# An encoder layer on one core: the down projection with tokens on the partitions, the up projection's products summed in their banks, group statistics in a transposes' bank

## The chip, the cores and the metric

One core of a Trainium2 chip runs the whole layer in one launch. The metric is the device time of one execution in microseconds (us). The kernel before was timed three times: 2064.53, 2067.25 and 2067.41 us, median 2067.25.

## The reference, cut to what matters

S = 512 tokens of D = 2048 channels; D_FF = 5632. All in float32. The change concerns the second half of the layer, the gated MLP and what ends it:

```
x = x + einsum("bsc,cd->bsd", mixed, w_out)          # out projection, residual
xn = rms_norm(x, ffn_norm_g)
up = einsum("bsd,df->bsf", xn, w_up)                 # 2048 -> 2 x 5632
up = depthwise_conv(up, ffn_dw_w, ffn_dw_b)          # width 3 over the tokens
gate, val = split(up, 2)
x = x + einsum("bsf,fd->bsd", silu(gate) * val, w_down)   # 5632 -> 2048
out = rms_norm(x, final_norm_g)
```

The first half (in projection, a convolution group and a neighbourhood attention group, each normalised, then the out projection) is touched in one place only: the banks in which two of its statistics are summed.

## The kernel before, in words

**Precision.** Every float32 operand is used as a sum of two parts, hi + lo, and a product is three matmuls: hi·hi, hi·lo, lo·hi. ACT makes the hi part (`whi`, L117, a copy of 1024 columns), DVE the lo part (`wlo`, L118, a subtraction). `weights()` runs a plan of weight units of 512 KB, `AHEAD` = 3 units ahead of their use: SP loads a unit into one of `NR` = 7 `raw` tiles (L112), then ACT and DVE split it. All engines take their instructions in order; a list scheduler fixes that order when the kernel is built, from priorities (the order of writing, shifted for the background `steps` that `tick` hands out) and from the tiles that are free. Nearly all intermediate tiles of 128x512 come from one pool of `NT` = 79 slots (`t2`), 56 of which hold the 28 combinations of the input through the whole MLP; a new tile waits until the last reader of the slot's old tile is done, be that reader an engine or a DMA.

**Up projection.** It goes through 44 blocks f of 128 gate and 128 value channels. For f >= 4 a block is seven products (a fast scheme for 2x2 blocks: seven half-size products instead of eight, over the halves of the channels and of the tokens). A product is 8 steps over k, each a matmul of 512 columns (L692, `whi` against [hi | lo] of 256 tokens) and one of 256 (L693, `wlo` against hi, into the upper half). So a bank of a product holds two halves, main and low. Each product has a bank of its own: products 0 to 5 go through the three "mm" banks, product 6 uses "po". ACT copies nine quarters of 256 columns out (`vv`, `pl`, L706) and DVE does eleven additions and two multiplications by the row statistic `rstd2` to make gate and value (L721 to L745, L788, L789). A conv of width 3 (`uy`, L780 to L782), silu (L791) and a product (L792) give the hidden block. Blocks f < 4 (`up_apart`) do the same with matmuls of 256.

**Down projection.** Four blocks make a chunk; there are 11. The hidden blocks of chunk c-1, split into `hh` and `hl`, wait in `pend` and are used while chunk c is made: a weight unit after product 3 of a block and one after product 6 (`down_units`). The weights are stationary and the tokens move: a unit holds the weights of two output blocks d, each takes 4 x 3 matmuls of 512 columns (L128 to L130) in a "tr" bank, ACT copies the bank to `pdc` (L812) and POOL adds it to the residual `xd[d]` in DRAM by an accumulating DMA of 256 KB (L813). Of a block's four such DMAs two follow product 3 and two product 6.

**The end.** In the last chunk the remaining eight d of `pend` run in one piece while the last weights are split into `dh`, `dl` (L839, L840) and the residual is loaded back into `x2`. Then `half(h0)` does the last chunk's contribution for the first 256 tokens, all 16 d, matmuls of 256 columns; `half(h1)` the other 256 tokens, with the statistic of the first half in between: 8 matmuls (L183) that sum the squares over the channels, which lie on the partitions, and 2 (L200) that spread the result over the partitions again. The first half's output is scaled and written in the shadow of the second half (`first_half`), the second half's after the last matmul.

**Statistics.** `rsqrt_steps` and the LayerNorm's mean (L389) take their bank from "sc", the bank pair of the attention scores.

Of the kernel before, what the change touches and what calls it, by code (L numbers as in the profile page):

```python
# [16 lines left out]
P = 128  # L17
D = 2048
# [22 lines left out]
H = S // 2  # L41
CH = 4
NCH = NF // CH
NT = 79
NR = 7
AHEAD = 3
# [13 lines left out]
         ("nag", NC_), ("g2", KD), ("fww", 2 * NF * 3), ("fwb", 2 * NF), ("g3", KD)]  # L60
# [9 lines left out]
def layer(ctx: ExitStack, tc: tile.TileContext, xT, w_in, w_v, w_out, w_up, w_down, par, tab, out):  # L70
# [20 lines left out]
    def t4(shape, name):  # L91

        return wpool.tile(shape, F32, tag="raw", name=name, bufs=NR)

# [70 lines left out]
    def sum_sq(acc, src, first, to=slice(0, S)):  # L165
        if first:
            nc.scalar.activation(acc, src, AF.Square)
        else:
            q = t2("sq")[:, to]
            nc.scalar.activation(q, src, AF.Square)  # L170
            nc.vector.tensor_add(acc, acc, q)

    def rsqrt_steps(accs, n, name, to=slice(0, S), keep=True, col=None):

        if not isinstance(accs, tuple):
            accs = accs,
        m = (to.stop - to.start) // P
        bank = lambda: (psa.tile([P, 2, S], F32, tag="sc", name="st")[:, 0] if col is None else
                        psa.tile([P, S], F32, tag="po", name="st"))
        ps = bank()  # L180
        for i in range(m):
            for acc in accs:
                nc.tensor.matmul(ps[:, i:i + 1], acc[:, to.start + i * P:to.start + (i + 1) * P], ones[:, 0:1],  # L183
                                 start=acc is accs[0], stop=acc is accs[-1])
        v, r, y = (sm.tile([P, S // P], F32, tag="rs" + c, name="rs" + c)[:, :m] for c in "vry")
        nc.vector.tensor_scalar(v, ps[:, :m], 1.0 / n, EPS, op0=ALU.mult, op1=ALU.add)
# [4 lines left out]
        nc.vector.scalar_tensor_tensor(y, y, 1.5, r, op0=ALU.add, op1=ALU.mult)  # L191
        if col is not None:
            nc.vector.tensor_copy(col, y)
# [6 lines left out]
        nc.tensor.matmul(ps[:, :m * P], ones, dg[:, :m * P], start=True, stop=True)  # L200
        if not keep:
            return ps[:, :m * P]
        res = t2(name)
        nc.scalar.activation(res[:, to], ps[:, :m * P], AF.Copy)
        return res

    def rsqrt_value(g):
        while True:
            try:
                next(g)  # L210
            except StopIteration as e:
                return e.value
# [165 lines left out]
    def group_a():  # L378
# [9 lines left out]
        ps = psa.tile([P, 2, S], F32, tag="sc", name="st")[:, 0]  # L388
# [194 lines left out]
    def after(d, ps):  # L583
# [26 lines left out]
        for c, f in enumerate((t4_, t1, t3, b11, t2_, b21, b22)):  # L610
            halves(f, c)
# [17 lines left out]
    def factors(f):  # L629
# [5 lines left out]
        def make(c):  # L635
            if c == 0:
                return load(A22)
            if c == 1:
                a["s"] = t4([P, U * P], "ws")
                add(a["s"], load(A21), a[A22])  # L640
            elif c == 2:
                add(a[A21], a[A21], load(A11))
                return a[A21]
            elif c == 3:
                return a[A11]
            elif c == 4:
                add(a["s"], a["s"], a[A11])
# [12 lines left out]
    def down_units(c, i, at):  # L660

        n = U // CH
# [4 lines left out]
        return {(1, 3): (0,), (1, 6): (2,), (2, 3): (4,), (2, 6): (6,), (3, 6): range(8, KD, n)}.get((i, at), ())  # L667

    def down_weights(f0, d0):
        return w_down[:, (f0 * KD + d0 * CH) * P:(f0 * KD + d0 * CH + U) * P]  # L670

    for c in range(NCH):
        for i in range(CH):
            for at, make in enumerate(factors(c * CH + i)):
                plan.append(make)
                for d0 in down_units(c, i, at):
                    plan.append(lambda c=c, d0=d0: unit(down_weights((c - 1) * CH, d0), U * P))
# [4 lines left out]
    def up(f, between):  # L682

        def product(c):

            w = weights()
            ps = (psa.tile([P, S], F32, tag="po", name="pu") if c == 6 else
                  psm.tile([P, S], F32, tag="mm", name="pu"))
            for k in range(U):
                hi, lo = (w[i][:, k * P:(k + 1) * P] for i in range(2))  # L690
                m = comb[c][k]
                wide = lambda: nc.tensor.matmul(ps, hi, m, start=k == 0, stop=k == U - 1)  # L692
                low = lambda: nc.tensor.matmul(ps[:, H:], lo, m[:, :H], start=False, stop=False)  # L693

                if k < U - 1:
                    wide()
                    i = low()
                else:
                    low()
                    i = wide()  # L700
            tick(i)
            between(c)
            return ps[:, :H], ps[:, H:]
# [4 lines left out]
        def pair(name):  # L708
            return t2(name).rearrange("p (i t) -> p i t", i=2)

        def both(x):
            return x.unsqueeze(1).broadcast_to([P, 2, H])


        vv, low = pair("vv"), pair("pl")
        for i in range(2):
            m, l = product(i)
            copy(vv[:, i], m)
            copy(low[:, i], l)
        m7, l = product(2)  # L720
        add(vv, vv, low)  # L721
        low = pair("pl")
        copy(low[:, 0], l)
        m1, l = product(3)
        copy(low[:, 1], l)
        uu, v = pair("uu"), pair("vl")
        u, u2 = uu[:, 0], uu[:, 1]
        add(u2, m7, low[:, 0])
        add(v, vv, both(u2))
        m6, l = product(4)  # L730
# [238 lines left out]
```

## Time and profile before

| | us |
|---|---|
| the three runs | 2064.53, 2067.25, 2067.41 |
| the profiled execution, its own time | 2063.7 |
| its span, first to last instruction | 2061.9 |
| TensorE (PE) busy | 2040.6 (99%) |
| VectorE (DVE) busy | 1652.3 (80%) |
| ScalarE (ACT) busy | 1057.5 (51%) |
| GpSimd (POOL) busy, nearly all of it issuing DMAs | 156.6 (8%) |
| mean granted TensorE clock | 0.997 |

The profiled execution is 3.55 us below the median of the three runs. Matmuls overlap, so the time that a matmul costs is the distance between the starts of two of them in the timeline, not its duration. The same goes, by about 0.1 us each, for DVE and ACT instructions that follow one another without a wait.

### The profile page before, as it was taken

Reading aid. Unit: us, or ns where it says so; the run is one execution under the profiler, and the core shown is the slowest. Engines: PE = TensorE matmul, PEld = TensorE weight load, DVE = VectorE, ACT = ScalarE, POOL = GpSimd, SP = SyncE. Lnnn points to the kernel's source line nnn. Section 1 sums busy time; section 2 is a strip of 40 time slices with the busy share of each in tenths; the row PEclk is TensorE's granted clock in tenths of the full one; section 3 lists DMA queues with packets and bytes.
Section 4 is the critical chain, followed back from the end, with each engine's and each line's share of the span. In section 5 each row is a group of like instructions: output and inputs, shape, how many; then the busy total and the mean of one; then the engine's idle time right before and its main releaser. Section 6 shows DMA issues by size and latency. Waiting matters only on the chain.

```text
span 2061.9 us, 28498 instructions
## 1 busy us (share of the span) xinstructions
PE 2040.6 (99%) x10746; PEld 1726.8 (84%) x10746; DVE 1652.3 (80%) x2285; ACT 1057.5 (51%) x1714; POOL 156.6 (8%) x186
## 2 busy tenths in 40 slices
PE   9999999999999999999999999999999999999997
PEld 7888888777888998888888888888888888888887
DVE  7798893975577898888888888788788887889876
ACT  7223423466536555555555555555554554555562
POOL 0000000000001001111111111111111111110110
PEclk9999999999999999999999999999999999999998
DMA  6532234325447435555465555555555565554572
GB/s 242 163 103 92 93 115 151 103 72 184 136 144 187 117 123 141 126 143 144 117 150 143 131 135 143 135 131 143 136 134 143 129 144 142 131 137 123 148 210 82
DMA packets 103338, 281.68 MB, mean 137 GB/s; under 512 B 12064, under 2 KB 16672, under 8 KB 103200
## 3 DMA queue, kind: packets, MB, share of 16 engines
q1 hardware_dynamic: 77840, 233.70, 35.7%
q0 software_dynamic: 25216, 46.15, 14.9%
q8 instruction: 85, 1.39, 0.3%
q14 instruction: 53, 0.43, 0.1%
q10 hardware_dynamic: 144, 0.01, 0.0%
HBM read 223.18 MB, written 56.62 MB: 136 GB/s over the span
## 4 chain that ended last, share of the span: by engine, by line
PE 89%; DVE 4%; DMA 3%; issue 2%; ACT 1%; POOL 0%; SPq 0%; DVEq 0%; POOLq 0%; ACTq 0%
PE pu L692 23%; PE pu L693 12%; PE pd L130 8%; PE pd L128 8%; PE pd L129 8%; PE pj L128 5%; PE pj L129 5%; PE pj L130 5%; PE po L128 2%; PE po L129 2%; PE po L130 2%; PE pv L315 1%; PE pv L314 1%; PE pv L316 1%; DMA sq<-sq 1%
## 5 line engine op out<-in xcount | busy, mean ns | idle before, releaser
L692 PE MATMUL pu<-xc,whi 128*128 128x512 f32 x2240 | 782.6, 397 | 0.2 <-ACT pl L706 0.2
L118 DVE TENSOR_TENSOR wlo<-raw,whi 128x1024 fp32r<-128x1024 f32 x364 | 444.7, 1222 | 247.6 <-ACT whi L117 232.1
L117 ACT ACTIVATE whi<-raw 128x1024 fp32r<-128x1024 f32 x364 | 385.1, 1059 | 470.5 <-PE pj L129 130.3
L693 PE MATMUL pu<-xc,wlo 128*128 128x256 f32 x2240 | 583.0, 281 | 0.0
L692 PEld LDWEIGHTS pu<-xc,whi 128*128 128x128 f32 x2240 | 407.8, 188 | 80.3 <-ACT pl L706 0.5
L693 PEld LDWEIGHTS pu<-xc,wlo 128*128 128x128 f32 x2240 | 422.8, 189 | 25.5
L130 PE MATMUL pd<-hh,wlo 128*128 128x512 f32 x640 | 248.9, 391 | 1.4 <-DVE wlo L118 1.4
L128 PE MATMUL pd<-hh,whi 128*128 128x512 f32 x640 | 249.8, 390 | 0.0
L129 PE MATMUL pd<-hl,whi 128*128 128x512 f32 x640 | 249.1, 389 | 0.0
L813 POOL DMA_DIRECT2D x2d<-pdc x160 | 139.6, 874 | 1174.0 <-ACT pdc L812 1072.1
L128 PE MATMUL pj<-xh,whi 128*128 128x512 f32 x512 | 200.5, 396 | 0.2 <-ACT xh L244 0.2
L129 PE MATMUL pj<-xl,whi 128*128 128x512 f32 x512 | 200.4, 391 | 0.1
L130 PE MATMUL pj<-xh,wlo 128*128 128x512 f32 x512 | 200.4, 391 | 0.0
L706 ACT ACTIVATE pl<-pu 128x256 f32<-128x256 f32 x280 | 105.1, 380 | 176.1 <-PE pu L692 176.1
L117 ACT ACTIVATE whi<-ws 128x1024 fp32r<-128x1024 f32 x132 | 139.8, 1059 | 68.5 <-PE pu L692 44.3
L372 DVE SCALAR_TENSOR_TENSOR y<-ch,prm,y 128x510 f32<-128x510 f32 (+14 forms) x240 | 172.0, 743 | 3.5
L118 DVE TENSOR_TENSOR wlo<-ws,whi 128x1024 fp32r<-128x1024 f32 x132 | 161.1, 1220 | 1.4 <-ACT whi L117 1.3
L130 PEld LDWEIGHTS pd<-hh,wlo 128*128 128x128 f32 x640 | 120.1, 188 | 30.0 <-DVE wlo L118 4.9
L812 ACT ACTIVATE pdc<-pd 128x512 f32<-128x512 f32 x160 | 93.9, 588 | 95.4 <-PE pd L130 95.4
L129 PEld LDWEIGHTS pd<-hl,whi 128*128 128x128 f32 x640 | 120.2, 188 | 25.7
L128 PEld LDWEIGHTS pd<-hh,whi 128*128 128x128 f32 x640 | 120.4, 188 | 21.8
L128 PEld LDWEIGHTS pj<-xh,whi 128*128 128x128 f32 x512 | 96.3, 188 | 25.0 <-issue 3.8
(176 smaller groups left out, 2913.7 us busy)
## 6 DMA issues: line engine op xcount, KB each, us to landing
raw<-in_w_up SPq DMA_DIRECT2D x176, 512.0 KB, 3.6
raw<-in_w_down SPq DMA_DIRECT2D x88, 512.0 KB, 3.6
x2d<-pdc POOLq DMA_DIRECT2D x160, 256.0 KB, 4.5
raw<-in_w_in SPq DMA_DIRECT2D x60, 512.0 KB, 3.7
raw<-in_w_out SPq DMA_DIRECT2D x32, 512.0 KB, 3.7
x<-in_xT SPq DMA_DIRECT2D x32, 256.0 KB, 4.3
raw<-in_w_v SPq DMA_DIRECT2D x16, 512.0 KB, 4.8
tab<-in_tab SPq DMA_DIRECT2D x32, 256.0 KB, 4.0
```

Source lines behind the costliest of these rows:

```text
L117: i = nc.scalar.activation(hi[:, :n], raw[:, :n], AF.Copy)
L118: j = nc.vector.tensor_sub(lo[:, :n], raw[:, :n], hi[:, :n].bitcast(F32))
L128: nc.tensor.matmul(ps, hi[:, a], mh, start=start, stop=False)
L129: nc.tensor.matmul(ps, hi[:, a], ml, start=False, stop=False)
L130: return nc.tensor.matmul(ps, lo[:, a], mh, start=False, stop=stop)
L314: nc.tensor.matmul(ps[i], xh, w[0][:, a], start=kk == 0, stop=False)
L372: nc.vector.scalar_tensor_tensor(y[:, a:b], h[:, a + j - PAD:b + j - PAD], prm[:, o + j:o + j + 1], y[:, a:b], op0=ALU.mult, op1=ALU.add)
L692: wide = lambda: nc.tensor.matmul(ps, hi, m, start=k == 0, stop=k == U - 1)
L693: low = lambda: nc.tensor.matmul(ps[:, H:], lo, m[:, :H], start=False, stop=False)
L706: nc.scalar.activation(to, ps, AF.Copy)
L812: nc.scalar.activation(t, ps, AF.Copy)
L813: nc.gpsimd.dma_start(xd[d], t, accum_op=ALU.add)
```

## The change: what it does

1. **Down projection turned round.** The hidden block is now the stationary operand (128 tokens of it), the weights move (512 columns), and a bank holds 128 tokens x 512 output channels. A unit is a quarter `a` of the output channels and half of a chunk's four blocks. Four banks (two "tr", "po", one "mm") are opened at the unit after product 3 and closed at the unit after product 6; only then come four `pdc` copies and four POOL DMAs in a row, into a new DRAM buffer `xq[a][i]` (i: token tile). The first of these writes does not add. The count of copies, DMAs and matmuls stays.
2. **The residual is turned** once, by `turn_residual`, a background step from chunk 1 on: 16 loads of `xd`, 16 DVE transposes in squares of 32, 32 writes of 64 KB in pieces of 256 bytes into `xt`, 16 loads of `xt`, and 16 accumulating POOL DMAs into `xq` (L844 of the new kernel).
3. **Up projection.** The order of the seven products changes so that products 0, 2, 4 and 6 go on in one "mm" bank and 1 and 3 in one half of the "sc" pair, product 5 in the other half. ACT copies five intermediate states of a bank, 512 columns each: `cx` after product 0 and after 2, `cz` after 1, `cy` after 4 and after 6. The next product of a bank has to wait for the copy. DVE does one addition of 1024 columns, three of 512 and one multiplication of 1024. The new tiles are four of 4 KB (`x4`), and `NT` falls from 79 to 71.
4. **Group statistics** use a "tr" bank.
5. **The end.** The eight groups left of `pend` (quarters 2 and 3) are added to `x2` by DVE straight from the bank. The last chunk goes token tile by token tile, four quarters each, matmuls of 512 columns; the last quarter of the last tile in two banks of 256. The squares are summed along the free axis by ACT's Square; the statistic of a token is one number per partition, so no matmul is needed. The four quarters are scaled by ACT (one) and DVE (three), and written in 4 DMAs of 256 KB per token tile.

The diff, cut to its core:

```
-NT = 79
+NT = 71
+NX = 4
 # rsqrt_steps, LayerNorm mean
-        ps = psa.tile([P, 2, S], F32, tag="sc", name="st")[:, 0]
+        ps = psa.tile([P, S], F32, tag="tr", name="st", bufs=2)
...
-            return {3: (4 * i,), 6: (4 * i + n,)}.get(at, ())
+            return {3: (2 * i,), 6: (2 * i + 1,)}.get(at, ())
...
     def up(f, between):
+        ps = psm.tile([P, S], F32, tag="mm", name="pu")
+        pair = psa.tile([P, 2, S], F32, tag="sc", name="pv")
+        x, y, z = x4([P, 2, S], "cx"), x4([P, 2, S], "cy"), t2("cz")
...
+        product(0, ps, True)
+        copy(x[:, 0], ps)
+        product(1, pair[:, 1], True)
+        copy(z, pair[:, 1])
+        product(2, ps, False)
+        copy(x[:, 1], ps)
+        product(3, pair[:, 1], False)
+        product(4, ps, False)
+        copy(y[:, 1], ps)
+        product(5, pair[:, 0], True)
+        add(y[:, 1], y[:, 1], z)
+        gv = x4([P, 2, S], "gv")
+        add(x, x, pair)
+        add(gv[:, :, :H], x[:, :, :H], x[:, :, H:])
+        product(6, ps, False)
+        copy(y[:, 0], ps)
+        add(gv[:, :, H:], y[:, :, :H], y[:, :, H:])
+        nc.vector.tensor_mul(gv, gv, rstd2[0].unsqueeze(1).broadcast_to([P, 2, S]))
...
+    def down(c, hs, us):
+        for u in us:
+            a, half = divmod(u, 2)
+            w = weights()
+            if not half:
+                banks.extend([psa.tile([P, S], F32, tag="tr", name="pd", bufs=2) for _ in range(2)] +
+                             [psa.tile([P, S], F32, tag="po", name="pd"), psm.tile([P, S], F32, tag="mm", name="pd")])
+            for i in range(NTT):
+                for k in range(2):
+                    down3(banks[i], w, k, hs, 2 * half + k, i, half == 0 and k == 0, half == 1 and k == 1)
+                if half:
+                    t = t2("pdc")
+                    nc.scalar.activation(t, banks[i], AF.Copy)
+                    if c:
+                        nc.gpsimd.dma_start(xq[a][i], t, accum_op=ALU.add)
+                    else:
+                        nc.gpsimd.dma_start(xq[a][i], t)
+            if half:
+                banks.clear()
...
+                nc.vector.transpose(t[:, :, e, :], xr.rearrange("p (b j) -> p b j", j=QF))
...
+                nc.sync.dma_start(xt[a].rearrange("(b i) f -> i b f", i=QF)[:, :, 2 * m * QF:2 * (m + 1) * QF],
+                                  t[p].rearrange("p b e j -> p b (e j)"))
...
+                t = t2("xr")
+                nc.sync.dma_start(t, xt[a][i * P:(i + 1) * P])
...
+                nc.gpsimd.dma_start(xq[a][i], t, accum_op=ALU.add)
...
+    for i in range(NTT):
+        pieces = [(a, slice(0, S)) for a in range(NQ)]
+        if i == NTT - 1:
+            pieces[-1:] = [(NQ - 1, slice(0, H)), (NQ - 1, slice(H, S))]
...
+            add(x, x, ps)
+            nc.scalar.activation(t2("sq")[:, c], x, AF.Square, accum_out=ssq[:, j:j + 1])
...
+            nc.vector.tensor_mul(fin[a][:, c], x, g3[a][:, c])
...
+        inv_sqrt(y, r, v)
+        for a in range(NQ):
+            to = out[i * P:(i + 1) * P, a * S:(a + 1) * S]
+            if a == 0:
+                nc.scalar.activation(fin[a], fin[a], AF.Copy, scale=y)
+                nc.scalar.dma_start(to, fin[a])
             else:
+                nc.vector.tensor_scalar(fin[a], fin[a], y, None, op0=ALU.mult)
+                nc.sync.dma_start(to, fin[a])
```

Three places in the order of the instructions. **ACT, at the turn from one ordinary block to the next, before** (`pdc`: down copies of the old block; `uy`: its conv; `vv`, `pl`: copies of the new block's products 0 and 1; the second `uy<-uy` is silu):

```order
L812 ACTIVATE pdc<-pd 128x512
L117 ACTIVATE whi<-raw 128x1024
L812 ACTIVATE pdc<-pd 128x512
L780 ACTIVATE uy<-g,prm 128x512
L780 ACTIVATE uy<-vl,prm,fwn 128x512
L706 ACTIVATE vv<-pu 128x256
L706 ACTIVATE pl<-pu 128x256
L117 ACTIVATE whi<-raw 128x1024
L791 ACTIVATE uy<-uy 128x512
```

The same place now:

```order
L812 ACTIVATE pdc<-pd 128x512
L124 ACTIVATE whi<-ws 128x1024
L812 ACTIVATE pdc<-pd 128x512 x3
L767 ACTIVATE uy<-gv,prm 128x512
L767 ACTIVATE uy<-gv,prm,fwn 128x512
L124 ACTIVATE whi<-raw 128x1024
L709 ACTIVATE cx<-pu 128x512
L124 ACTIVATE whi<-raw 128x1024
L776 ACTIVATE uy<-uy 128x512
L709 ACTIVATE cz<-pv 128x512
```

Four copies of the old block stand together ahead of the two `uy`, and the new block's first copy `cx`, for which product 2 has to wait, stands behind `uy`, `uy` and a `whi`.

**POOL's queue at the turn from block 31 to 32.** Before, the queue holds nothing but such rows in this stage, two to a weight unit:

```order
L813 DMA x2d_4844<-pdc 128x512
L813 DMA x2d_4845<-pdc 128x512
L813 DMA x2d_4846<-pdc 128x512
L813 DMA x2d_4847<-pdc 128x512
L813 DMA x2d_4848<-pdc 128x512
```

Now the rows come in fours, with the turned residual's rows (L844) among them:

```order
L844 DMA xq_5695<-xr 128x512
L814 DMA xq_5696<-pdc 128x512
L814 DMA xq_5697<-pdc 128x512
L844 DMA xq_5696<-xr 128x512
L814 DMA xq_5698<-pdc 128x512
L814 DMA xq_5699<-pdc 128x512
L844 DMA xq_5697<-xr 128x512
```

The second L844 row adds to the same `xq_5696` that the L814 row two places ahead of it adds to, so it waits for that one's landing, and the rows of `xq_5698` and `xq_5699` stand behind it.

**The end of the program.** PE, before: the last matmuls, then the statistic of the second half, squares summed over partitions and spread again:

```order
L128 MATMUL pd<-hh,dh 128x256
L129 MATMUL pd<-hl,dh 128x256
L130 MATMUL pd<-hh,dl 128x256
L183 MATMUL st<-ones,acc_18257 128x1
L183 MATMUL st<-ones,sq 128x1
L183 MATMUL st<-ones,acc_18257 128x1
L183 MATMUL st<-ones,sq 128x1
L200 MATMUL st<-dg,ones 128x256
```

Now PE ends with matmuls, and what follows stands on ACT (and, beside it, on DVE):

```order
L915 ACTIVATE sq,rsq<-x_17070 128x512
L915 ACTIVATE sq,rsq<-x_17071 128x512
L915 ACTIVATE sq,rsq<-x_17072 128x256 x2
L182 ACTIVATE rsr<-rsv 128x1
L927 ACTIVATE fin<-fin,rsy 128x512
L928 DMA out_Q<-fin 128x512
```

The two matmul steps of the statistic are gone from the chain; a square root per token and one scaling remain ahead of the last write.

More of the change, by code (lines that the diff above doesn't have):

```diff
@@ L168, in sum_sq, with inv_sqrt @@
         else:
-            q = t2("sq")[:, to]
+            q = t2("sq")
             nc.scalar.activation(q, src, AF.Square)
             nc.vector.tensor_add(acc, acc, q)
[L173 to L186, printed above, removed]
+    def inv_sqrt(y, r, v):
         nc.scalar.activation(r, v, AF.Sqrt)
@@ L199, in rsqrt_steps @@
         ps = bank()
-        nc.tensor.matmul(ps[:, :m * P], ones, dg[:, :m * P], start=True, stop=True)
-        if not keep:
-            return ps[:, :m * P]
+        nc.tensor.matmul(ps, ones, dg, start=True, stop=True)
         res = t2(name)
-        nc.scalar.activation(res[:, to], ps[:, :m * P], AF.Copy)
+        nc.scalar.activation(res, ps, AF.Copy)
         return res
[L207 to L212, printed above, removed]
     xs, x1 = [], []
```

293 lines of the change are left out of this document (140 added, 153 removed).

## The prediction

> **What bounds the kernel now.** I read the busy times first, then the chain of work that ended last, then what PE waited for.
>
> ```profile
> span 2061.9 us, 28498 instructions
> PE 2040.6 (99%) x10746; PEld 1726.8 (84%) x10746; DVE 1652.3 (80%) x2285; ACT 1057.5 (51%) x1714; POOL 156.6 (8%) x186
> PE 89%; DVE 4%; DMA 3%; issue 2%; ACT 1%; POOL 0%; SPq 0%; DVEq 0%; POOLq 0%; ACTq 0%
> PE st L183 <- DVE su L469: 2.4, 1, 2.4
> PE st L200 <- DVE dg L197: 1.9, 1, 1.9
> PE pd L130 <- DVE wlo L118: 1.4, 8, 0.2
> ```
>
> PE is the bound from start to end: it has no wait above 2.4 us, and those it has before its last matmul sum to a few us. So DVE's and ACT's work costs nothing today, and to relieve them earns nothing. A change can gain only in two ways: less matmul time, or a shorter end after the last matmul. It can lose by any wait that it puts in front of a matmul, and there are 40 blocks in which it could do so.
>
> The up and down stage, one window of about one block:
>
> ```profile
> 1200.00:1231.00 31.00, 31.00 (x164) 26.50 (x163) 24.82 (x31) 16.59 (x26) 3.49 (x4) 1.00 0.57 138
> 1226.30 0.39 PE L129 MATMUL pd<-hl,whi 128*128 128x512 f32 x1
> 1229.93 0.39 PE L130 MATMUL pd<-hh,wlo 128*128 128x512 f32 x1
> 1230.15 0.39 PE L692 MATMUL pu<-xc,whi 128*128 128x512 f32 x1
> 1231.20 0.40 PE L692 MATMUL pu<-xc,whi 128*128 128x512 f32 x1
> ```
>
> The columns of the first row are PE, weight loads, DVE, ACT, POOL, then the clock and the DMA share: PE 31 of 31 us, DVE 24.8, ACT 16.6, DMA engines 57%. From the first of these starts to the second lie 16 matmuls: 3.63/16 = 0.227 us for 512 columns. From the third to the fourth, three pairs of a wide and a low matmul: 0.35 us a pair, so a product of 8 pairs takes 2.8 us.
>
> **1. Matmul time in the stage: nothing.** A chunk's down projection is 16 x 12 = 192 matmuls of 512 columns in both kernels; that weights and tokens swap places does not change 0.227. A product keeps its 8 pairs. DVE's eleven additions and two multiplications go, four additions and the multiplications of 512 columns, seven of 256:
>
> ```profile
> L721 DVE TENSOR_TENSOR vv<-vv,pl 128x512 f32<-128x512 f32 x1 | 0.7, 685 | 0.0
> L728 DVE TENSOR_TENSOR uu<-pu,pl 128x256 f32<-128x256 f32 x1 | 0.4, 416 | 0.0
> L640 DVE TENSOR_TENSOR ws<-raw 128x1024 f32<-128x1024 f32 x1 | 1.2, 1216 | 0.0
> ```
>
> That is 6 x 0.69 + 7 x 0.42 = 7.1 us a block; new are two of 1024 and three of 512, 2 x 1.22 + 3 x 0.69 = 4.5. DVE falls from 24.8 to some 22 of the window's 31 us; ACT's nine copies of 256 columns become five of 512, about as long together. Both lie beside PE: worth 0.
>
> **2. Matmuls of the last bank: -3.8 us.**
>
> ```profile
> 1998.81 0.28 PE L128 MATMUL pd<-hh,dh 128*128 128x256 f32 x1
> 1998.92 0.28 PE L129 MATMUL pd<-hl,dh 128*128 128x256 f32 x1
> 1999.04 0.28 PE L130 MATMUL pd<-hh,dl 128*128 128x256 f32 x1
> 2023.28 0.28 PE L183 MATMUL st<-ones,acc 128*128 128x1 f32 x2
> 2028.21 0.67 PE L200 MATMUL st<-dg,ones 128*128 128x256 f32 x2
> 2046.22 0.28 PE L130 MATMUL pd<-hh,dl 128*128 128x256 f32 x1
> ```
>
> From 1998.81 to 2046.34 (the last start plus 0.12) PE works 47.5 us on 384 matmuls of 256 columns, at 0.12 each, and on ten matmuls of the first half's statistic. Now it is 180 of 512 at 0.227 and 24 of 256 at 0.12, with no statistic: 40.8 + 2.9 = 43.7.
>
> **3. The end after the last matmul: -6.8 us.**
>
> ```profile
> 2046.54 0.42 DVE L871 TENSOR_TENSOR x<-x,pd 128x256 f32<-128x256 f32 x1 [0.67 <-PE pd L130]
> 2046.99 0.42 ACT L876 ACTIVATE sq<-x 128x256 f32<-128x256 f32 x1 [0.67 <-DVE x L871]
> 2048.43 0.16 DVE L186 TENSOR_SCALAR rsv<-st 128x2 f32<-128x2 f32 x1 [1.14 <-PE st L183]
> 2049.46 0.16 DVE L191 SCALAR_TENSOR_TENSOR rsy<-rsy,rsr 128x2 f32<-128x2 f32 x1
> 2051.57 4.79 DVE L861 SCALAR_TENSOR_TENSOR fin<-x,prm,st 128x256 f32<-128x256 f32 x12 [1.43 <-ACT rb L900]
> 2053.06 5.00 SPq L862 DMA_DIRECT2D out_T<-fin  x8
> DMA to landing us min/median/max: 2.2/2.7/3.3
> 2054.00:2060.00 6.00, 0.00 (x0) 0.00 (x0) 2.35 (x7) 0.00 (x0) 0.41 (x1) 0.50 1.04 341
> ```
>
> From the last matmul's start (2046.22) to the span's end are 15.7 us. Addition and square end at +1.2 and stay, with perhaps 0.2 for reading the sum out. The small steps from 2048.43 to 2049.62 (1.2 us) stay, but follow at once: the statistic is there at about +2.7, where it was at +3.4 and then went through two more matmuls, so that the scaling began at 2051.57. Then 2 MB were written; the last row shows that the DMA engines were full from 2054 to 2060, at 341 GB/s. Now 1 MB goes out: 3.1 us at that rate. ACT's scaling takes about 0.6 (a copy of 512 columns), DVE's three 0.4 to 0.7 each (the rows for 256 and 512 columns above), so the last DMA is issued near +4.8, lands 2.7 later, and 1.4 us follow a landing as now (8 issues ending at 2058.1, landing near 2060.5, end 2061.9). Sum +8.9: -6.8. Bounds: -5.5 if a landing takes 3.3 and the read-out is slow, -7.5 if the four writes overlap fully.
>
> **4. Statistics in a "tr" bank: 0.** The wait of 2.4 us in the first fence is L183 in attention: its "sc" bank was still to be read by a softmax that DVE did late, for want of a table from DRAM. That wait goes. What is late next: the statistic's own steps run on the same DVE, and PE's following matmul (L207 of the new kernel) stands 14 places earlier than L200 did, so it waits for DVE instead. Between -2.4 (the wait goes entirely) and +1 (DVE's steps after it cost more than they did); I take 0, since the cause, DVE held by the table, is untouched.
>
> **5. New waits in the stage: +5.3 us.** Call T the start of a block's product 0. Product 2 must wait for `cx`, ACT's copy after product 0; it may start at T + 5.6. Likewise 3 waits for `cz`, 4 for `cx`, 6 for `cy`; each copy has the 2.8 us of the product between, or a down unit of 24 x 0.227 = 5.4 beside it. In an ordinary block ACT comes to `uy` at T + 0.9, behind the last `pdc`, and after `uy`, `uy`, `whi` (rows below) the first `cx` ends at about T + 4; the other copies have as much to spare: free. Three places are not ordinary.
>
> *(a) uy behind a DMA.* With `NT` at 71, in the last block of most chunks (7, 11, ... 39) the slots for `uy` are those of the first two `pdc` tiles, which come free when POOL's DMA has landed. `uy` stands ahead of `cx` on ACT.
>
> ```profile
> 1199.49 1.06 ACT L117 ACTIVATE whi<-raw 128x1024 fp32r<-128x1024 f32 x1 [1.89 <-PE pd L129]
> 1200.46 0.58 ACT L812 ACTIVATE pdc<-pd 128x512 f32<-128x512 f32 x1
> 1200.94 0.80 ACT L780 ACTIVATE uy<-g,prm 128x512 f32<-128x512 f32 x1
> 1201.64 0.80 ACT L780 ACTIVATE uy<-vl,prm,fwn 128x512 f32<-128x512 f32 x1
> x2d<-pdc POOLq DMA_DIRECT2D x4, 256.0 KB, 4.7
> DMA to landing us min/median/max: 3.9/4.7/5.7
> DMA to landing us min/median/max: 4.8/6.2/7.6
> ```
>
> Token tiles end 1.36 us (6 x 0.227) apart, so the second bank is done at T - 2.7; behind `whi` its copy ends at about T - 1.65, where its DMA is issued. The second `uy` starts at the landing; `uy`, `whi` and `cx` then take 0.70 + 0.97 + 0.59, with the hand-overs 2.4. Product 2 is late by landing - 1.65 + 2.4 - 5.6 = landing - 4.85. The two landing rows are block 1200 to 1231 (issues 3.5 us or more apart) and the last chunk, where issues come closer. Four now come 0.88 apart; the second has one ahead of it. I take 5.1, near the first row's 4.7: 0.25 us in each of 8 blocks, 2.0. Bounds: 0 (3.9) and 2.75 (7.6) each, 0 to 22.
>
> *(b) Block 31.* Here a row of the turned residual stands behind the second `pdc` row on POOL, waits for the first one's landing, and holds a slot that `uy` needs: two landings in a row from about T - 3.2, 9 to 9.4 us, so late by -3.2 + 9.2 + 2.4 - 5.6 = 2.8; with 3.9 twice 1.4. I take 2.0. The two DMAs queued behind it only free tiles later.
>
> *(c) ACT's order.* In block 40, without down units, ACT has the second `cx` ahead of `cz`, so product 3 starts behind product 2's end plus a copy: +0.9. In the first blocks of chunks 2 to 9 it is the same, but six down matmuls (1.36 us) stand between products 2 and 3 and cover it but for 0 to 0.3: +0.4 in all.
>
> *(d) More DMAs.* The residual's 64 moves by SP (16 loads of 256 KB, 32 writes of 64 KB, 16 loads) and 16 accumulates lie in blocks 25 to 37, beside weight loads that come three units ahead.
>
> ```profile
> q1 hardware_dynamic: 864, 3.15, 32.8%
> q0 software_dynamic: 610, 1.12, 24.2%
> q1 hardware_dynamic: 77840, 233.70, 35.7%
> vt<-vd SPq DMA_DIRECT2D x64, 64.0 KB, 1.9
> ```
>
> The first two rows are the window of 31 us (packets, MB, share), the third the whole run. Four accumulates take 24.2% of 31 us, 1.9 us of all engines each; plain loads take 32.8% for 3.15 MB, 3.2 us a MB, 0.85 for 256 KB and 0.2 for 64 KB. The new traffic is 16 x 1.9 + 32 x 0.85 + 32 x 0.2 = 64 us in 12 blocks (some 370 us), 17%: 0.57 becomes 0.74, still not full. SP's queue stops where it waits for an `xr` slot, but what stands behind it, weight loads, has three units of lead (over 8 us) against a landing of some 4. I take 0; the price when the cover is gone is below.
>
> The 64 KB row is of longer pieces; the new writes go in 256 pieces of 256 bytes each. The Trainium skill, "DMA: Bandwidth & Descriptors", section "Specifications", says that pieces under 512 B miss the full rate, as the engine then reads and writes back. No run here shows such a write. By a doubling of its 0.2 us a write would take 0.4, 6 us of DMA time in all, and the sum would stay; what it does if a piece is as dear as a packet is a rival.
>
> **Sum.** -3.8 - 6.8 + 0 + 2.0 + 2.0 + 1.3 = **-5.3 us**: 2063.7 becomes 2058.4 for an execution like the profiled one. Against the runs' median, 3.55 higher, 2062.0. I predict against the median.
>
> **Rivals.**
> - *No new wait at all.* Landings stay under 4.85 (the median of all 160 is 4.5) and block 31's two are quick: only steps 2 and 3 are left with 0 to 3 us against them. 2056.5 to 2059.8. For it: PE's almost unbroken record of before. Against: the burst.
> - *Slower: the burst's landings decide.* If a second landing in a burst takes 6.2 us or more, as in the last chunk, (a) is 8 x 1.35 = 10.8, and with 7.6 it is 22; the same delay enters (b) once for each of its two landings (+3), and (c) stays 1.3. That is +17 to +28 against -10.6: 2074 to 2085. It turns slower by more than a measurement can tell when the waits pass 14.7 us, about 1.4 us in each of the nine blocks. For it: four DMAs of 1.9 us arrive within 3.5 us. Against: nothing stands ahead of the first, and only the first two matter.
> - *The gain is eaten.* Waits of 8 to 14.7 us, by landings near 5.8 or other slots that the smaller pool makes late in every block: 2064.8 to 2071.
> - *The pieces of 256 bytes.* An average packet on SP's queue takes 0.357 x 16 x 2061.9 / 77840 = 0.15 us of one engine. If each piece takes two such, a write is 256 x 0.3 / 16 = 4.8 us of all engines, 155 us for 32, 42% of the stretch: 0.57 + 0.15 + 0.42 = 1.14 passes 1, weights come late by some 14% of 370 us: 2062 + 52 = 2114. One packet's time each leaves it under 1, and free. That a short piece costs twice, once to read and once to write back, is what the Trainium skill's "DMA: Bandwidth & Descriptors", section "Specifications", would make of it.
>
> **How the numbers follow.** Forecast (waits 3 to 8 us, 2059.8 to 2064.8) 0.42; no wait 0.24; eaten 0.13; slower by the burst 0.17; pieces 0.04. A measurement of this kernel can tell about 0.2%, 4.1 us, from no change. Faster by more (under 2063.1): the whole of the second case and two thirds of the first, 0.52. Within: the rest of the first and nearly all of the eaten, 0.26. Slower: 0.22. The range 2056 to 2075 takes in the first, second and fourth cases and the near end of the burst; beyond it lie the pieces, most of the burst's bad end and a little below, some 0.18.
>
> **What the profile after would show.** Step 2: from the first matmul of the last bank to the last 43.7 us, and no L183 among them. Step 3: some 8.9 us from the last matmul to the end, one MB of writes. Step 4: a wait of L207 on DVE of 1 to 3 us in place of L183's. Step 5: PE waits on `cx` in blocks 7, 11, ... 39 of 0 to 1 us, a 2 us one in block 31, one of 0.9 in block 40, and no wait of ACT's `whi` on a `raw` DMA. The prediction is wrong if PE waits on a copy in every block, or if the landing of the second `pdc` is above 6.

## The result and the profile after

| | before | after |
|---|---|---|
| median of 4 runs, us | 2066.71 (2064.53 to 2067.41) | 2048.56 (2048.00 to 2049.33) |
| profiled execution, us | 2063.7 | 2049.33 |
| its span, us | 2061.9 | 2047.1 |

The ratio is 0.9914, with a 95% interval of 0.9897 to 0.9931: faster by 18 us, between 14 and 21. The prediction was 2062.0 with a range of 2056 to 2075: right in its direction, 13 us off, and outside its range.

The page of the changed kernel: busy times, chain of work that ended last, and what PE waited for (total us, times, longest).

```profile
span 2047.1 us, 27645 instructions
PE 2033.3 (99%) x10546; PEld 1714.4 (84%) x10546; DVE 1583.9 (77%) x1965; ACT 1042.8 (51%) x1546; POOL 155.2 (8%) x190
PE 66%; issue 26%; POOL 3%; DMA 2%; ACT 1%; DVE 1%; SPq 0%; POOLq 0%; DVEq 0%; ACTq 0%
PE pu L694 <- ACT cx L709: 3.0, 4, 1.6
PE st L387 <- DVE acc L384: 0.3, 1, 0.3
```

PE is still the bound. The statistic's wait of 2.4 us in the attention is gone; new are four waits on `cx`, 3.0 us in all, in the up and down stage. (The 26% "issue" in the chain are stretches in which PE's next matmul has no releaser in the records; it is no idle time, PE is busy 99%.)

**Where the 14.8 us of span went.** I cut both executions at five landmarks of PE, each taken at its start: the LayerNorm mean (`st<-acc`), the last transpose of the attention (`trp`), the first 512-column matmul of the up stage (`pu`), the first matmul of the last bank (`dh`), and the last matmul. The landmarks are rows such as these, the views of the tiles of before (count, duration in ns, first and last start):

```profile
L483 PE MATMUL trp<-ident,s x128: 270/272/330, 157.2 to 557.2; 128*128 128x128 f32 x128
L692 PE MATMUL pu<-xc,whi x2240: 387/398/504, 769.2 to 1976.8; 128*128 128x512 f32 x187
```

and of after:

```profile
L481 PE MATMUL trp<-ident,s x128: 270/272/331, 156.9 to 551.3; 128*128 128x128 f32 x128
L694 PE MATMUL pu<-xc,whi x1280: 387/398/504, 763.3 to 1972.8; 128*128 128x512 f32 x183
```

| stretch, us | before | after | difference | predicted |
|---|---|---|---|---|
| start to LayerNorm mean | 411.6 | 411.4 | -0.2 | |
| to the last transpose (rest of the attention) | 145.6 | 139.9 | **-5.7** | 0 |
| to the up stage | 212.0 | 212.0 | 0 | |
| up and down stage | 1229.6 | 1231.5 | +1.9 | +5.3 |
| last bank | 47.4 | 43.5 | -3.9 | -3.8 |
| after the last matmul | 15.7 | 8.8 | -6.9 | -6.8 |

Steps 2 and 3 came out as worked. What was missed is the attention stretch, and the up stage lost less than I had put against it. The end of the changed kernel, the timeline from the last addition:

```profile
2038.64 0.42 DVE L914 TENSOR_TENSOR x<-x,pd 128x256 f32<-128x256 f32 x1
2039.09 0.42 ACT L915 ACTIVATE sq<-x 128x256 f32<-128x256 f32 x1 [0.92 <-DVE x L914]
2039.41 0.19 ACT L915 ACTIVATION_READ_ACCUMULATOR sq<-x 128x1 f32 x1
2039.63 0.16 DVE L922 SCALAR_TENSOR_TENSOR rsv<-rsq,rsy 128x1 f32<-128x1 f32 x1
2040.84 0.72 ACT L927 ACTIVATE fin<-fin,rsy 128x512 f32<-128x512 f32 x1 [0.81 <-DVE rsy L186]
2041.36 1.38 SPq L931 DMA_DIRECT2D out_Q<-fin  x3
```

From the last matmul's start, 2038.32, the scaling starts at +2.5 (predicted +2.7), and the three DMAs of SP are out by 2042.7; the span ends at +8.8.

**The four new waits**, from PE's timeline:

```profile
1352.56 0.50 PE L694 MATMUL pu<-xc,whi 128*128 128x512 f32 x1 [0.36 <-ACT cx L709]
1600.09 0.50 PE L694 MATMUL pu<-xc,whi 128*128 128x512 f32 x1 [1.65 <-ACT cx L709]
1723.43 0.50 PE L694 MATMUL pu<-xc,whi 128*128 128x512 f32 x1 [0.27 <-ACT cx L709]
1880.59 0.50 PE L694 MATMUL pu<-xc,whi 128*128 128x512 f32 x1 [0.69 <-ACT cx L709]
```

By their starts (some 30.7 us a block from 763.3, where block 4 begins) they stand at product 2 of blocks 23, 31 and 35, places that the prediction named, and in block 40 at product 4, which runs ahead of product 3 there; the prediction had put that one at product 3. The one of 1.65 us shows the mechanism whole, in the timeline of ACT and PE:

```profile
1596.40 0.82 ACT L767 ACTIVATE uy<-gv,prm 128x512 f32<-128x512 f32 x1 [0.83 <-DMA xq<-pdc]
1598.74 0.81 ACT L767 ACTIVATE uy<-gv,prm,fwn 128x512 f32<-128x512 f32 x1 [1.53 <-DMA xq<-xr]
1599.46 0.58 ACT L709 ACTIVATE cx<-pu 128x512 f32<-128x512 f32 x1
1600.09 0.50 PE L694 MATMUL pu<-xc,whi 128*128 128x512 f32 x1 [1.65 <-ACT cx L709]
```

The second `uy` waits for the slot that the turned residual's accumulating DMA still reads; `cx` stands behind `uy`, and PE's product 2 behind `cx`.

### The profile page after: what moved, and what is told of

Its sections match the earlier page's. It is cut to its first block, busy times and chain, and to the rows that moved or that the text cites. A ratio compares the mean times of both kernels' runs of the same rounds, so it can differ in the third digit from the quotient of the medians.

```text
span 2047.1 us, 27645 instructions
## 1 busy us (share of the span) xinstructions
PE 2033.3 (99%) x10546; PEld 1714.4 (84%) x10546; DVE 1583.9 (77%) x1965; ACT 1042.8 (51%) x1546; POOL 155.2 (8%) x190
## 3 DMA queue, kind: packets, MB, share of 16 engines
q1 hardware_dynamic: 97296, 246.28, 39.2%
q0 software_dynamic: 25344, 48.25, 15.7%
## 4 chain that ended last, share of the span: by engine, by line
PE 66%; issue 26%; POOL 3%; DMA 2%; ACT 1%; DVE 1%; SPq 0%; POOLq 0%; DVEq 0%; ACTq 0%
PE pu L694 7%; PE pj L135 6%; PE pj L136 6%; PE pj L137 5%; PE pv L694 5%; PE pd L795 4%; PE pd L797 4%; PE pd L796 4%; PE pu L696 4%; PE po L135 3%; PE po L136 3%; PE po L137 3%; PE pv L696 3%; POOL xq L814 3%; PE pv L313 1%
## 5 line engine op out<-in xcount | busy, mean ns | idle before, releaser
L694 PE MATMUL pu<-xc,whi 128*128 128x512 f32 x1280 | 466.2, 398 | 3.2 <-ACT cx L709 3.0
L694 PE MATMUL pv<-xc,whi 128*128 128x512 f32 x960 | 348.9, 398 | 0.0
L696 PE MATMUL pu<-xc,wlo 128*128 128x256 f32 x1280 | 333.0, 281 | 0.0
L696 PEld LDWEIGHTS pu<-xc,wlo 128*128 128x128 f32 x1280 | 241.5, 189 | 14.0
L696 PE MATMUL pv<-xc,wlo 128*128 128x256 f32 x960 | 249.9, 281 | 0.0
L797 PE MATMUL pd<-whi,hl 128*128 128x512 f32 x640 | 249.4, 390 | 0.0
L796 PE MATMUL pd<-wlo,hh 128*128 128x512 f32 x640 | 249.1, 389 | 0.0
L795 PE MATMUL pd<-whi,hh 128*128 128x512 f32 x640 | 246.8, 390 | 0.0
L694 PEld LDWEIGHTS pv<-xc,whi 128*128 128x128 f32 x960 | 180.9, 188 | 34.2 <-ACT cz L709 2.0
L696 PEld LDWEIGHTS pv<-xc,wlo 128*128 128x128 f32 x960 | 181.2, 189 | 10.7
L814 POOL DMA_DIRECT2D xq<-pdc x136 | 118.7, 873 | 837.6 <-ACT pdc L812 827.6
```

What stands on the lines that cost most here:

```text
L694: main = lambda: nc.tensor.matmul(to, hi, m, start=first and k == 0, stop=k == U - 1, skip_group_check=not first)
L696: low = lambda: nc.tensor.matmul(to[:, H:], lo, m[:, :H], start=False, stop=False, skip_group_check=not first)
L795: nc.tensor.matmul(ps, h, hi, start=start, stop=False)
L796: nc.tensor.matmul(ps, h, lo, start=False, stop=False)
L797: return nc.tensor.matmul(ps, l, hi, start=False, stop=stop)
L814: nc.gpsimd.dma_start(xq[a][i], t, accum_op=ALU.add)
```

## The experiments

Theory A, formed from the table: the statistics' bank alone shortened the attention. With the score pair as its bank, a statistic stands between two score rows; PE, in order, must wait until the softmax has read the pair, and no new score row can start before the statistic is read. Theory B: the attention got shorter by another order that came with the smaller pool of slots, and the bank is worth at most the 2.4 us that the waits named.

**1. The bank alone, in the kernel before.** The edit stands in two places, the LayerNorm mean and, as a lambda, `rsqrt_steps`; here the first.

```
-        ps = psa.tile([P, 2, S], F32, tag="sc", name="st")[:, 0]
+        ps = psa.tile([P, S], F32, tag="tr", name="st", bufs=2)
```

> The kernel before with one edit: the statistics' bank is a transposes' bank, as in the changed kernel. Theory A (the bank of the statistics by itself is what shortened the attention stage, because a statistic in the score pair stands between two pairs of score rows): the first 512-column matmul of the up stage starts 5 to 6 us earlier than 769.2, so at 763 to 764, and the time falls by 5 to 6 us against the kernel before. Theory B (the stage got shorter by the smaller pool of slots, or by another order that came with it, and the bank is worth at most the 2.4 us wait that the waits name): a start at 767 to 769 and 0 to 2.4 us.

Measured: 2058.18 us median of 4 against 2066.23 of the kernel before measured beside it, ratio 0.9959 (0.9944 to 0.9973): 8 us faster, between 6 and 12. In its profile the attention stretch is 140.7 us and the up stage starts at 765.0:

```profile
L483 PE MATMUL trp<-ident,s x128: 270/272/331, 157.6 to 552.6; 128*128 128x128 f32 x128
L692 PE MATMUL pu<-xc,whi x2240: 387/398/500, 765.0 to 1972.8; 128*128 128x512 f32 x187
```

The start is 4.2 us earlier, between what the two theories expected, but the stretch is 4.9 us shorter and the time 6 us or more, where B allowed 2.4. Theory A holds, B falls; the size in the medians is above what I expected from the one profile of before.

**2. The statistics back in the score pair, in the changed kernel** (the same edit the other way).

> The changed kernel with the statistics put back into the score pair. Theory A: 5 to 6 us slower than the changed kernel (2048.6), some 2054, first up matmul of 512 columns near 769, with PE's wait of about 2.4 us at the convolution group's statistic back. Theory B: within 2.4 us of the changed kernel, up matmul at 763 to 766.

Measured: 2054.82 us (2053.62 to 2056.12), 6.3 above the changed kernel; up stage from 768.3, attention stretch 144.3. What PE waited for in the attention:

```profile
PE st L195 <- DVE s L461: 2.1, 1, 2.1
PE st L387 <- DVE acc L384: 0.6, 1, 0.6
PE trp L481 <- ACT s L469: 0.3, 1, 0.3
```

The wait at the statistic is back. A holds from this side too, and the smaller pool, which this kernel has, is not the cause. One thing that neither theory named changes with the bank: the list scheduler then builds another order, of SP's queue too (see step 4 below).

**3 and 4. Only one kind of statistic back.** First the root-mean-square ones (`rsqrt_steps`), then the LayerNorm mean.

> The changed kernel with only the root-mean-square statistics (three in this stage) back in the score pair, the mean of the LayerNorm left in the transposes' bank. Theory A in its form that the root-mean-square statistics matter, since they hold the pair for 5 to 7 us between two matmul steps: 5 to 6 us slower than the changed kernel, as if all were put back. If the mean mattered as well: half of it or less. Theory B: 0 to 2.4 us.

> The changed kernel with only the LayerNorm mean back in the score pair. Theory A in the form above: no change against the changed kernel (within 0.5 us), up matmul at 763 to 764. If the mean matters: 2 us or more slower. Theory B: 0.

Measured: 2051.61 (2050.86 to 2054.67) and 2050.22 (2049.31 to 2051.45); attention stretches 143.2 and 141.0, against 139.9 with none and 144.3 with both. So my narrower form fell: by the profiles the root-mean-square statistics carry most of it (3.3 us of 4.4) and the mean about 1 us, which lies near the spread of single profiles; by the medians it is 3.1 and 1.7 us of 6.3. That the mean has a share is likely; its size is not shown.

**5. The turned residual in another order of quarters.**

```
-        for a in range(NQ):
+        for a in reversed(range(NQ)):
             for i in range(NTT):
```

> The changed kernel with the turned residual added in the opposite order of quarters, so that no such row stands on POOL one or two places behind the down row that adds to the same tile. If PE's wait of 1.65 us in block 31 comes from that row's wait for a landing, it goes (under 0.4 us left there), and the time falls by 1 to 2 us against the changed kernel, 2047. If it comes from the landing of the down copies themselves, the wait stays between 1 and 2 us and the time with it.

Measured: 2047.18 us (2045.98 to 2048.58). PE's waits in the stage:

```profile
PE pu L694 <- ACT cx L709: 1.1, 3, 0.7
```

The longest is now 0.7, that of block 40; the 1.65 us wait is gone and the stage took 1228.9 us in place of 1231.5. In five executions with the old order of quarters (the changed kernel, experiments 2, 3, 4 and 11) it took 1230.5 to 1232.5. The wait did come from POOL's order. The median is 1.4 us below that of the changed kernel, but the kernel before, measured beside it, was also 1.6 lower (2065.08); as a gain in time it is not shown.

**6. No residual.** Line `steps.append(turn_residual())` left out: the output lacks the residual.

> The changed kernel without the turning of the residual: its 64 moves, 16 transposes and 16 accumulating DMAs are left out, so the output lacks the residual. If the residual costs only block 31's wait: 1.5 to 2 us faster than the changed kernel, 2047. If its DMA traffic (pieces of 256 bytes among it) holds weights back as well, more than 3 us, and DVE's waits for a weight unit's landing, 40 us in the changed kernel, fall below 20.

Measured: 2046.94 us (2045.85 to 2047.61), stage 1229.2. The kernel before was again 2065.08 beside it, so the median tells no gain either. The stage has the length of experiment 5, 1 to 3 us below those with the residual in its old order: the residual costs about its one wait, and nothing else that can be told. DVE's waits for weights stay:

```profile
DVE ws L638 <- DMA raw<-in_w_up: 19.2, 28, 1.2
DVE raw L644 <- DMA raw<-in_w_up: 14.2, 24, 1.0
```

33 us in place of 41: they are not the residual's doing, and PE does not see them.

**7. Slots of their own for the down copies.**

```
-NT = 71
+NT = 68
-                    t = t2("pdc")
+                    t = tp.tile([P, S], F32, tag="pdc", name="pdc", bufs=3)
```

> The changed kernel with three slots of their own for the down copies and 68 for the rest, so that no conv tile waits for a down copy's landing. By the price in the prediction, late by landing minus 4.85 us, with landings of 4.9 in the mean: PE's waits on cx in blocks 23 and 35 (0.63 us together) go, block 40's 0.69 stays, the time falls by 0.5 to 1 us. Rival: the fourth copy of a burst now waits on ACT for the first one's landing, ahead of uy, and PE waits more, 1 us or more in many blocks.

Measured: 2057.89 us (2057.82 to 2060.68), 9 us slower than the changed kernel, where I expected a gain; the stage took 1239.3. The rival held in part. The landing is now waited for by the fourth copy, in 33 places (first row, ACT), but little of that reaches PE: its waits are the last two rows, at four places, and the larger ones, on `cz` in blocks 22 and 30, come from slots that tiles of the residual hold (second row for the one of 4.6 us).

```profile
ACT pdc L812 <- DMA xq<-pdc: 39.3, 33, 2.3
ACT cz L709 <- DMA xq<-xr: 4.7, 1, 4.7
PE pv L694 <- ACT cz L709: 6.4, 2, 4.6
PE pu L694 <- ACT cx L709: 2.1, 2, 1.4
```

**8. Each DMA of the down copies twice,** the first into a scratch buffer `scr` (its declaration is left out here).

```
                     if c:
+                        nc.gpsimd.dma_start(scr[i], t, accum_op=ALU.add)
                         nc.gpsimd.dma_start(xq[a][i], t, accum_op=ALU.add)
                     else:
+                        nc.gpsimd.dma_start(scr[i], t)
                         nc.gpsimd.dma_start(xq[a][i], t)
```

> The changed kernel with each of the down projection's accumulating DMAs issued twice, first into a scratch buffer; the output is unchanged. It tests the rival that the burst's landings decide. By the price in the prediction the second copy's slot comes free some 2.5 to 3.5 us later (one more issue of 0.88 on POOL for each of the two, and a landing that is about 2 us longer with twice the traffic ahead): product 2 late by 2 to 3 us in each of nine blocks, 18 to 27 us slower than the changed kernel, 2067 to 2076. If those landings are not on PE's path: under 4 us.

Measured: 2133.12 us (2127.82 to 2135.66): 85 us slower than the changed kernel, some four times what I expected. The stage grew from 1231.5 to 1313.1. PE's waits there, and the times from issue to landing of the DMAs of `pdc`:

```profile
PE pv L694 <- ACT cz L709: 34.3, 8, 7.5
PE pu L694 <- ACT cx L709: 21.8, 12, 4.3
DMA to landing us min/median/max: 2.3/5.5/9.0
```

Of the 12 waits on `cx`, eight are the expected ones, 20 us in all, at product 2 of blocks 11, 15, ... 39. What I had not counted are eight waits on `cz`, up to 7.5 us: `cz` comes from the same pool, and with the slots out longer it takes one that a down copy holds. So the burst's landings do decide once their cover is gone, and more steeply than the one term I had for it. The named waits are 56 us of the 82. Most of the rest is the clock: behind the longer waits it was granted at half (see the last section).

**9 and 10. The kernel before, twice more,** for where its spread lies.

> The kernel before, unchanged, profiled again, to see where its spread from run to run lies (2063 to 2070 us so far, the profiled execution 2063.7). If it lies in the stage where the statistics stand in the score pair: the first 512-column up matmul starts later than 769.2 by about as much as the time is above 2063.7, and all later stages keep their lengths within 0.5 us. If it is spread over all stages: less than half of it there.

> As the run before, a second execution of the same kernel, with the same expectations.

Measured: 2065.58 and 2066.64 us. The stretches of six executions, the first three and the last with the statistics in the score pair:

| us | to mean | attention | to up | up, down | last bank | end |
|---|---|---|---|---|---|---|
| before | 411.6 | 145.6 | 212.0 | 1229.6 | 47.4 | 15.7 |
| before, again | 410.6 | 147.7 | 212.3 | 1229.7 | 47.4 | 16.1 |
| before, third | 411.6 | 148.3 | 212.3 | 1229.7 | 47.4 | 15.6 |
| experiment 1 | 411.9 | 140.7 | 212.4 | 1229.8 | 47.3 | 15.6 |
| after | 411.4 | 139.9 | 212.0 | 1231.5 | 43.5 | 8.8 |
| experiment 2 | 411.7 | 144.3 | 212.3 | 1231.2 | 43.5 | 8.8 |

The third ended 3.0 us of span later than the first and its up stage started 3.0 later; for the second it is 1.9 and 1.4. So the spread of these three lies mostly in the attention, and the one profile that I worked from was its best case: the bank is worth 5.7 us against that profile and about 8 against the others. That is also part of why the median moved by 18 us and the profiled span by 15.

What spreads there is the granted clock. The windows around the statistic's wait, of the first, the second and the third execution (two rows; the last three columns are clock, DMA share and GB/s):

```profile
430.00:445.00 15.00, 12.65 (x77) 9.83 (x76) 7.45 (x18) 8.61 (x21) 0.00 (x0) 1.00 0.33 105
430.00:445.00 15.00, 12.78 (x71) 9.78 (x70) 7.52 (x19) 8.25 (x18) 0.00 (x0) 0.89 0.31 105
430.00:445.00 15.00, 13.01 (x67) 10.20 (x67) 7.73 (x19) 8.94 (x21) 0.00 (x0) 0.84 0.32 105
445.00:470.00 25.00, 25.00 (x128) 19.52 (x125) 17.18 (x24) 18.95 (x27) 0.00 (x0) 0.96 0.20 58
```

The wait itself is about as long in all three (2.4, 2.2 and 2.0 us). Behind it the clock stayed full in the first, was at half for 3.4 us in the second and for 6.8 us in the third. PE was busy all that time, so about 1.7 and 3.4 us went there; the stretches are 2.1 and 2.7 us longer. Without the wait (experiment 1, the changed kernel) the clock stays at 1.00 in this stretch.

**11. The last quarter in one bank.**

```
-        if i == NTT - 1:
+        if False:
             pieces[-1:] = [(NQ - 1, slice(0, H)), (NQ - 1, slice(H, S))]
```

> The changed kernel with the last quarter of the last token tile in one bank of 512 columns in place of two of 256. After the last matmul the addition takes 0.69 in place of 0.42 and the square 0.63 in place of 0.42, with an overlap of about 0.1; the matmuls gain 0.15: 0.3 to 0.6 us slower by the profile's last part (9.2 from the last matmul's start to the end, in place of 8.8), which the median may not tell. If the end is set by the writes alone: no difference in that part.

Measured: 2048.61 us (2048.28 to 2051.58), no difference in the median. By the profile the last bank took 43.3 us in place of 43.5 and the end 9.4 in place of 8.8: the halves are worth about 0.4 us, as expected.

## Why the prediction was wrong, by its steps

**Step 4 failed.** It says: "I take 0, since the cause, DVE held by the table, is untouched." The runs showed 5.7 us in the profiles and 8 us in the medians of experiment 1. The step looked at the one wait that the profile named and asked whether its releaser would be faster. The question was what PE could do meanwhile. Before, the statistic's matmuls could not start until DVE had read the scores; its timeline there:

```profile
436.87 0.69 DVE L463 SCALAR_TENSOR_TENSOR s<-sc,tab 128x512 f32<-128x512 f32 x1 [3.44 <-DMA tab<-in_tab]
440.37 1.02 PE L183 MATMUL st<-ones,acc 128*128 128x1 f32 x8 [2.35 <-DVE su L469]
473.56 0.67 PE L453 MATMUL sc<-k,q 64*128 64x256 f32 x2 [0.57 <-DVE s L463]
489.12 0.84 PE L483 MATMUL trp<-ident,s 128*128 128x128 f32 x4 [0.32 <-ACT s L471]
```

And the timeline after, PE's and DVE's rows:

```profile
432.58 1.05 PE L195 MATMUL st<-ones,acc 128*128 128x1 f32 x8
434.91 0.69 DVE L461 SCALAR_TENSOR_TENSOR s<-sc,tab 128x512 f32<-128x512 f32 x1 [1.08 <-DMA tab<-in_tab]
440.17 0.70 PE L207 MATMUL st<-dg,ones 128*128 128x512 f32 x1
```

DVE still waits for the table, but the statistic stands on PE directly behind the score matmuls, 8 us earlier, ahead of that wait, and its second step (L207), which I had expected to wait 1 to 3 us, comes without a wait (in experiments 1 and 4 with 0.4 and 0.6 us). The waits at 473 and 489 go as well; as I read it, since the score pair is free for the next rows. In the profile of before, the waits that PE names in this stretch sum to 3.5 us (2.4, 0.6, 0.3, 0.3); in the profile after there is none. At matching rows the lead is 3.1 us at the transposes behind the first statistic (449.9 us in the one execution, 446.6 in the other, each less the start of the mean), and the whole 5.7 at the `po` row of 516.0 (510.1). Some 0.5 of the 2 us that no wait names are two projection matmuls that now run ahead of the mean, where PE had waited for it; what makes up the rest I have not shown. The bounds that I gave, -2.4 to +1, were those of the one wait and not of the resource.

Nor was the cause quite untouched. With the mean's bank the scheduler also changed the order of SP's queue: the table's load was issued at 430.63 in place of 432.42, and DVE had the table 2.0 us earlier. Experiment 3, with only the mean in the new bank, has the early load (430.42), experiment 4, with only the mean in the old one, the late load (432.61). Since the attention of experiment 4 is still only 141.0 us, the early load can be worth about 1 us at most; the place of the root-mean-square statistics is worth more.

**The base was a second error.** The sum was made against a profile 3.55 us below the median and then moved to the median unchanged, as if the difference would stay. The changed kernel's profile lies 0.8 us above its median, so the base makes 4.3 us of the 13.4. By experiments 9 and 10, 2 to 3 us of that lay in the very stretch that step 4 dealt with: the half clock that can follow the wait. The other 9.1 us are the attention, 5.7, and the stage of step 5, 3.4.

**Step 5 was right in mechanism and too dear.** +5.3 was put down; the waits are 3.0 us and the stage's growth 1.9, since PE's small waits on `wlo` of before (1.4 us) went at the same time. By term: (a) `uy` behind a landing, 2.0 predicted, 0.63 measured, in two blocks of eight. ACT's waits and the median landing, us:

```profile
ACT uy L767 <- DMA xq<-pdc: 15.2, 16, 1.7
xq<-pdc POOLq DMA_DIRECT2D x152, 256.0 KB, 4.9
```

`uy` did wait for landings in 16 places, so the slots are as read from the order, but with 4.9 in the median most of it was covered, as "landing minus 4.85" says; I took 5.1. (b) block 31: 2.0 against 1.65, shown by experiments 5 and 6. (c) 1.3 against 0.69, all of it in block 40 and at product 4: the order there is 2, 4, 3, so the product that waits for the copy of product 2 is another, by the same mechanism.

In (d), and ahead of the prediction, I had the residual's writes as 64 KB, and in blocks 25 to 37. They are 128 KB (512 pieces of 256 bytes each), in the first half of the stage; only the loads of `xt` and the accumulates lie later:

```profile
L834 SPq DMA_DIRECT2D xt<-xt x32: 325/424/1467, 778.5 to 1338.7; - x32
L841 SPq DMA_DIRECT2D xr<-xt x16: 326/327/383, 1409.7 to 1725.8; - x16
1400.00:1430.00 30.00, 30.00 (x158) 25.58 (x157) 22.40 (x24) 15.97 (x21) 5.21 (x6) 1.00 0.75 164
```

The DMA share is 0.75 in this window and 0.70 over 1409 to 1726 us, where all of these loads lie. The 0.74 of the working came near it partly by luck, since it had put traffic there that lies elsewhere. As it said, the engines were not full, and experiment 6 shows no wait of PE from it.

**Steps 1, 2 and 3 were right**: PE's pace is unchanged, and DVE has room, with 22.4 of 30 us busy in that window; the last bank and the end came within 0.1 us of their terms.

**The rivals.** No case reached below 2056.5 us, for none had a gain in the attention; that the direction was right rests on steps 2 and 3. "No new wait" comes nearest, with 3 us of waits, but not for its reason. "Slower by the burst" is a real mechanism, as experiment 8 shows, yet it begins above the landings of this kernel. The short pieces cost nothing that can be told (experiment 6). Two slips of the working change nothing: 14.7 us over nine blocks are 1.6 us each, not 1.4, and the "fourth" case that the range takes in is the third, the eaten gain.

## What to carry to other kernels

A named wait of 2.4 us can be the visible part of a longer stretch: where a small step borrows a buffer from a pipeline, ask what that pipeline loses while the buffer is away, and not only what the step waits for. Cut the executions at landmarks of the bounding engine; a table of six stretches showed what the list of waits did not. Profile the kernel before more than once where its runs spread by as much as the terms of the sum, and read the granted clock of the stretch that spreads: a wait of 2 us had a price of its own there and, in two of three executions, a second one behind it.

## What the runs showed of the hardware that was not expected

**The granted clock can fall to half behind a pause of PE of 2 us.** In experiment 8 it was 0.99 where PE was busy 331 of 336 us and 0.94 where it was busy 178 of 200 (columns: PE, weight loads, DVE, ACT, POOL, clock, DMA share, GB/s):

```profile
764.00:1100.00 336.00, 331.10 (x1723) 281.77 (x1722) 253.92 (x266) 177.50 (x236) 59.41 (x80) 0.99 0.70 176
1500.00:1700.00 200.00, 177.59 (x879) 149.43 (x878) 130.58 (x135) 92.67 (x125) 47.34 (x54) 0.94 0.81 172
```

The trace's clock records say more: in this stage the clock was at half in eleven stretches of 3.4 to 10.2 us, 57.9 us in all, and PE was busy in 46.4 of them. That is some 23 us of lost work, most of the 26 that the named waits leave. Between the start of the program and its last bank, such a stretch began in or right behind each of the ten waits of PE of 2.5 us or more in the thirteen profiles, behind four of ten waits between 1.9 and 2.5 us (two of them in experiments 9 and 10), and behind none of the shorter ones. What decides among the middle ones no run separates.

**Writes in pieces of 256 bytes were not dear in engine time.** By the queue's shares (39.2% of 2047.1 us against 35.7% of 2061.9, times 16 engines) the 19,456 packets that SP's queue has more took 1061 us of one engine, 0.055 us each, against the 0.15 of an average packet before. 16,384 of them are the pieces; if all of the 1061 us were theirs, it would be 0.065 us a piece. But the 32 writes of 128 KB landed in 4.0 us in the median, where 256 KB writes of `x2d` in the same execution landed in 2.0. Nothing waited for them here.
